# A decoder layer on one core: final norm's column sums addend by addend, one output tile on another queue, and a new order of all instructions

## The chip, the cores and the metric

The kernel runs on one core of a Trainium2 chip. Times are device microseconds (us) of a whole execution; the profile's own span is from the first to the last instruction. The engines are TensorE (PE, with its weight loads as PEld), VectorE (DVE), ScalarE (ACT), GpSimd (POOL) and SyncE (SP), which only issues transfers; ACT and POOL issue transfers as well, in the same row as their other instructions.

## The reference, cut to what matters

One layer over 512 tokens with model width 1024, float32 throughout:

```python
h = h + 0.5 * swiglu(rmsnorm(h, ffn1_norm), ffn1_w_gate, ffn1_w_up, ffn1_w_down)
proj = rmsnorm(h, mix_norm) @ w_in                # u, v, z, xbc, dt
ya = rmsnorm(chunked_spatial_gating(gelu(u), gelu(v), ...), gm_out_norm)
yb = mamba2_mixer(z, xbc, dt, ...)                # causal conv, SSD in chunks of 128, gated norm
h = h + concatenate([ya, yb], -1) @ w_out
h = h + 0.5 * swiglu(rmsnorm(h, ffn2_norm), ffn2_w_gate, ffn2_w_up, ffn2_w_down)
gate = sigmoid(rmsnorm(h, ple_norm) @ ple_w_gate + ple_b_gate)
h = h + gate * (p @ ple_w_proj)
return rmsnorm(h, final_norm)                     # y * rsqrt(mean(y*y) + eps) * gain, per token
```

## The kernel before, in words

The layer is held feature by feature: `h` is eight tiles of 128 features x 512 tokens. Large products are made in float32r, of which the trace records one pass for each matmul and not two as for float32: each float32 operand is split into a high and a low float32r part (`whi`, `wlo` for weights; ACT casts the high part, DVE subtracts it to get the low one), and a product is three float32r matmuls, high by high, high by low, low by high. In the FFNs and the mixer, products are 256 columns (half the tokens) or 512 wide. Small products stay float32: the column sums over features against a tile of ones, the transposes against `ident`, the causal convolution and the state-space part of the mixer (`convin`, `m`, `u`). PE's row is a mixture of the two.

The end of the kernel: the gate of the per-layer embeddings is a product for each of eight feature tiles d. For the last three, d = 5, 6, 7 (`BY_HALF = 3`), it is made by halves of the tokens, A and B, 256 each (`gate_half`, line 1842). Behind each, DVE and ACT apply the sigmoid and the embedding, add to `h`, square it (`sq`), and scale `h` by the final gain. `factors` (line 1850) adds four squares (that of d 0 to 4 together, `total`, which is the tile `ssum`, and d 5, 6, 7) over the features by 128x1 matmuls into one PSUM bank, and makes the factors of a half (`rlast`) from it with a square root on ACT and some short DVE steps. `rows_out` (line 1864) transposes `h` back to rows, four 128x128 transposes to a bank, eight banks in all; ACT evicts the banks with q = 0, DVE those with q = 1, each scaling by `rlast`, and ACT's queue sends ACT's tiles, SP's queue DVE's.

No engine's order follows from the code. All instructions are recorded first, cut into units (a PE unit is the run of matmuls into one bank), and issued in the order of the string `ORDER`, a list of the units' numbers. So what stands next to what on each engine, and each place in a queue, is set by that list, and every recorded instruction has the line of `issue` (1905) in the profile. `b` and `a` are PSUM banks.

Of the kernel before, what the change touches and what calls it, by code (L numbers as in the profile page):

```python
# [76 lines left out]
for _name, _w in _VECS:  # L77
# [211 lines left out]
def layer_kernel(ctx: ExitStack, tc: tile.TileContext, a: dict, out: bass.AP):  # L289
# [93 lines left out]
    def sm_ps(at=None):  # L383
        return bank()
# [1457 lines left out]
    def gate_half(i, tok):  # L1842
# [4 lines left out]
        gained(d, tok)  # L1847
        return sq

    def factors(tok, sqs):  # L1850

        chunks = range(tok.start // P, tok.stop // P)
        ps = sm_ps()
# [24 lines left out]
    for i in range(BY_HALF):  # L1878
        squares_of[0].append(gate_half(i, halves[0]))
# [133 lines left out]
```

## Time and profile before

| | before |
|---|---|
| median of 3 runs | 1074.15 us (1074.07 to 1074.2) |
| profiled execution | 1073.36 us |
| its span | 1071.6 us |
| TensorE's granted clock, mean | 0.999 |
| PE busy | 1062.1 us (99%) |
| DVE busy | 817.0 us (76%) |
| ACT busy | 559.5 us (52%) |
| POOL busy | 75.2 us (7%) |

The profiled execution is one run by itself; its time is the span and what lies around it. PE's busy time counts a matmul from its start to its modelled end, and successive matmuls overlap, so that 99% says that PE has no holes, not that it works at its peak.

### The profile page before, as it was taken

How to read it: one execution, taken by the hardware profiler on the slowest of the kernel's cores; microseconds unless marked ns; L12 is line 12 of the kernel's file. 1: busy time of each engine (PE TensorE's matmuls, PEld its weight loads, DVE VectorE, ACT ScalarE, POOL GpSimd, SP SyncE). 2: the span in 40 equal slices, each digit the busy share in tenths (PEclk: the TensorE clock that was granted, in tenths of full speed). 3: DMA queues.
4: the chain of work that ended last, by engine and by line, in shares of the span. 5: the costliest groups of instructions: out<-in, count | busy, mean ns of one | idle time of the engine just before them, and what ended most of it. 6: DMA issues, size and time to landing. Idle time of an engine off the chain costs nothing.

```text
span 1071.6 us, 17611 instructions
## 1 busy us (share of the span) xinstructions
PE 1062.1 (99%) x7151; PEld 965.0 (90%) x7151; DVE 817.0 (76%) x1169; ACT 559.5 (52%) x781; POOL 75.2 (7%) x95
## 2 busy tenths in 40 slices
PE   9999999999999999999999999999999999999997
PEld 7899999999998878998999888999999999999887
DVE  6978685867577879999999767988667575857866
ACT  7655344444444537887865435654434343534545
POOL 1100000100000000000100000010100000000000
PEclk9999999999999999999999999999999999999999
DMA  9876765766452236777855435786755757633412
GB/s 322 238 202 166 196 181 193 196 181 174 99 154 82 65 113 146 187 201 175 212 135 130 138 98 137 218 236 186 204 143 155 211 144 197 181 115 85 139 53 79
DMA packets 52209, 173.27 MB, mean 162 GB/s; under 512 B 5920, under 2 KB 6176, under 8 KB 52128
## 3 DMA queue, kind: packets, MB, share of 16 engines
q1 hardware_dynamic: 33696, 116.93, 32.1%
q0 software_dynamic: 12256, 44.57, 23.1%
q10 hardware_dynamic: 6176, 10.65, 3.4%
q8 instruction: 56, 0.92, 0.3%
q14 instruction: 25, 0.20, 0.1%
HBM read 167.86 MB, written 4.26 MB: 161 GB/s over the span
## 4 chain that ended last, share of the span: by engine, by line
PE 99%; DVE 0%; ACT 0%; issue 0%; DVEq 0%; ACTq 0%
PE b L1905 81%; PE a L1905 18%; DVEq L2008 0%; DVE o L1905 0%; ACT m L1905 0%; ACT b L1905 0%; DVE tmp L1905 0%; DVE h L1905 0%; DVE ones L410 0%; DVE nv L1905 0%; ACTq L1905 0%
## 5 line engine op out<-in xcount | busy, mean ns | idle before, releaser
L1905 PE MATMUL b<-xfb,whi 128*128 128x256 f32 (+1 forms) x1704 | 297.5, 278 | 0.7 <-ACT b L1905 0.7
L1905 PEld LDWEIGHTS b<-xfb,whi 128*128 128x128 f32 x1704 | 261.0, 188 | 6.0 <-ACT b L1905 0.9
L1905 PE MATMUL b<-xfb,wlo 128*128 128x256 f32 (+1 forms) x852 | 237.2, 278 | 0.0
L1905 ACT CAST whi<-raw 128x1024 fp32r<-128x1024 f32 (+1 forms) x131 | 136.0, 1041 | 146.4 <-PE b L1905 109.7
L1905 DVE TENSOR_TENSOR wlo<-raw,whi 128x1024 fp32r<-128x1024 f32 (+1 forms) x130 | 156.8, 1212 | 28.7 <-ACT whi L1905 25.8
L1905 PEld LDWEIGHTS b<-xfb,wlo 128*128 128x128 f32 x852 | 159.9, 188 | 0.5
L1905 PE MATMUL b<-xfa,whi 128*128 128x256 f32 (+1 forms) x696 | 124.0, 281 | 0.0
L1905 PEld LDWEIGHTS b<-xfa,whi 128*128 128x128 f32 x696 | 107.0, 188 | 2.5 <-DVE xfa L1905 0.2
L1905 PE MATMUL b<-xfa,wlo 128*128 128x256 f32 (+1 forms) x348 | 97.8, 281 | 0.0
L1905 ACT CAST whix<-rawd 128x1024 fp32r<-128x1024 f32 (+1 forms) x40 | 39.4, 986 | 88.5 <-PE a L1905 47.9
L1905 DVE TENSOR_TENSOR wlo<-rawb,whi 128x1024 fp32r<-128x1024 f32 x51 | 62.1, 1220 | 23.2 <-ACT whi L1905 23.1
L1905 ACT CAST whi<-rawb 128x1024 fp32r<-128x1024 f32 x51 | 53.3, 1049 | 48.8 <-PE b L1905 39.7
L1905 PE MATMUL b<-m,whi 128*128 128x512 f32 x224 | 69.6, 392 | 0.0
L1905 DVE TENSOR_TENSOR wlox<-rawd,whix 128x1024 fp32r<-128x1024 f32 (+1 forms) x40 | 45.7, 1143 | 27.0 <-ACT whix L1905 26.9
L1905 PEld LDWEIGHTS b<-xfa,wlo 128*128 128x128 f32 x348 | 65.4, 188 | 0.5
L1905 PE MATMUL b<-xb,whi 128*128 128x256 f32 (+1 forms) x280 | 62.2, 318 | 0.0
L1905 PE MATMUL b<-ghi,wlox 128*128 128x512 f32 x156 | 61.4, 394 | 0.0
L1905 PE MATMUL b<-glo,whix 128*128 128x512 f32 x156 | 61.2, 392 | 0.0
L1905 PE MATMUL b<-ghi,whix 128*128 128x512 f32 x156 | 60.7, 389 | 0.0
L1905 PE MATMUL a<-ghi,wlox 128*128 128x512 f32 x140 | 55.2, 394 | 0.0
L1905 PE MATMUL a<-glo,whix 128*128 128x512 f32 x140 | 54.9, 392 | 0.0
L1905 PE MATMUL a<-ghi,whix 128*128 128x512 f32 x140 | 54.4, 389 | 0.0
(294 smaller groups left out, 2223.8 us busy)
## 6 DMA issues: line engine op xcount, KB each, us to landing
raw<-in_ffn_gu SPq DMA_DIRECT2D x57, 512.0 KB, 5.4
rawd<-in_ffn_down SPq DMA_DIRECT2D x40, 512.0 KB, 4.4
raw<-in_ffn_gu POOLq DMA_DIRECT2D x32, 512.0 KB, 7.7
rawb<-in_ffn_gu SPq DMA_DIRECT2D x31, 512.0 KB, 6.1
s<-in_ffn_gu SPq DMA_DIRECT2D x21, 512.0 KB, 5.5
s<-in_ffn_gu POOLq DMA_DIRECT2D x21, 512.0 KB, 8.5
raw<-in_w_out SPq DMA_DIRECT2D x16, 512.0 KB, 3.6
raw<-in_w_in SPq DMA_DIRECT2D x13, 512.0 KB, 3.7
```

The costliest lines, as they stand in the source:

```text
L1905: getattr(getattr(real, engine), what)(*(real_of(x) for x in args), **{k: real_of(x) for k, x in kw.items()})
```

## The change

It does three things. First, the column sums: each half gets its bank ahead of the loop, `total` is added at once, and each gate half's square is added behind its product (`column_sums`); `factors` only makes the factors. Second, `rows_out` sends the last tile that DVE evicts (chunk 3, q = 1) from ACT's queue and not from SP's. Third, `ORDER` is replaced as a whole by another list that a search has found, in which a change from float32 to float32r (or back) on PE carried a charge. The list's numbers tell a reader nothing and are left out, but for its first line:

```diff
 ORDER = (
-    "1-2 5-7 9-10 13 12 11 3 14 16 18 20 24 15 17 19 0 25 21 77 26 41 27 29 42 38 37 39-40 34 8 35 43 33 "
...
+    "1-2 5-7 9-10 13 12 11 0 3 14 16 18 24 20 15 17 19 25 21 26 41 78 27 29 42 37-38 40 39 8 43 32 36 "
...
@@ -1847,16 +1848,14 @@
         gained(d, tok)
         return sq
 
-    def factors(tok, sqs):
-
-        chunks = range(tok.start // P, tok.stop // P)
-        ps = sm_ps()
-        for j, sq in enumerate([total[:, tok]] + sqs):
-            for i in range(len(chunks)):
-                nc.tensor.matmul(
-                    ps[:, i : i + 1], sq[:, i * P : (i + 1) * P], ones[:, 0:1], start=i + j == 0,
-                    stop=j == len(sqs) and i == len(chunks) - 1, skip_group_check=True,
-                )
+    def column_sums(ps, sq, first, last):
+        for i in range(2):
+            nc.tensor.matmul(
+                ps[:, i : i + 1], sq[:, i * P : (i + 1) * P], ones[:, 0:1], start=first and i == 0,
+                stop=last and i == 1, skip_group_check=True,
+            )
+
+    def factors(ps):
         rt = sb("rlast", (P, 2))
         rsqrt_by_table(rt, ps[:, :2], 1.0 / D, (P, 2))
         return rt
@@ -1872,17 +1871,16 @@
                     nc.scalar.activation(o, ps, AF.Copy, scale=rt[:, i : i + 1])
                 else:
                     nc.vector.tensor_scalar(o, ps, rt[:, i : i + 1], None, ALU.mult)
-                (nc.sync if q else nc.scalar).dma_start(out[c * P : (c + 1) * P, q * T : (q + 1) * T], o)
-
-    squares_of = [[], []]
+                (nc.sync if q and c < NC - 1 else nc.scalar).dma_start(out[c * P : (c + 1) * P, q * T : (q + 1) * T], o)
+
+    sums = [sm_ps(), sm_ps()]
+    for k, tok in enumerate(halves):
+        column_sums(sums[k], total[:, tok], True, False)
     for i in range(BY_HALF):
-        squares_of[0].append(gate_half(i, halves[0]))
-    for i in range(BY_HALF):
-        if i == BY_HALF - 1:
-            r_a = factors(halves[0], squares_of[0])
-        squares_of[1].append(gate_half(i, halves[1]))
-    rows_out(halves[0], r_a)
-    rows_out(halves[1], factors(halves[1], squares_of[1]))
+        for k, tok in enumerate(halves):
+            column_sums(sums[k], gate_half(i, tok), False, i == BY_HALF - 1)
+    rows_out(halves[0], factors(sums[0]))
+    rows_out(halves[1], factors(sums[1]))
```

The instructions are the same in number and kind on every engine. Three places show how the list moves them.

On PE in the mixer, in the convolution's part, before: a group of four `convin` matmuls (float32; each number after a name is that of a buffer) stands behind float32r products, with two float32r matmuls against `onesr` behind it.

```order
L1905 MATMUL b_6001<-xb_3482,whi_5911 128x256 x2
L1905 MATMUL b_6001<-xb_3482,wlo_5932 128x256
L1905 MATMUL b_6026<-convin_5070,m_5463 128x128
L1905 MATMUL b_6026<-convin_5070,m_5581 128x128
L1905 MATMUL b_6026<-convin_5070,m_5390 128x128
L1905 MATMUL b_6026<-convin_5070,m_5388 128x128
L1905 MATMUL b_6031<-tmp_5779,onesr_73 128x512
L1905 MATMUL b_6031<-tmp_5936,onesr_73 128x512
```

Now, from the same place: the two `onesr` matmuls come first, and seven groups of `convin` stand in one piece, 28 matmuls without a float32r product among them.

```order
L1903 MATMUL b_5995<-xb_3477,whi_5909 128x256 x2
L1903 MATMUL b_5995<-xb_3477,wlo_5929 128x256
L1903 MATMUL b_6020<-tmp_5873,onesr_73 128x512
L1903 MATMUL b_6020<-tmp_5935,onesr_73 128x512
L1903 MATMUL b_6023<-convin_5155,m_5468 128x128
L1903 MATMUL b_6023<-convin_5155,m_5391 128x128
...
L1903 MATMUL b_6096<-convin_5519,m_5706 128x128
L1903 MATMUL b_6096<-convin_5519,m_5700 128x128
L1903 MATMUL b_5995<-xb_3474,whi_6040 128x256 x2
L1903 MATMUL b_5995<-xb_3474,wlo_6059 128x256
```

Before, these seven groups stood in pieces of 4, 12 and 12, each behind 24 products or more. Another four `convin` follow later at the same place in both.

On PE at the very end, before: behind the last product come the sums of half A, then 16 transposes (left out), then the sums of half B, then the rest.

```order
L1905 MATMUL b_10793<-x_10224,wlo_10691 128x256
L1905 MATMUL b_10854<-ones_71,ssum_10670 128x1 x2
L1905 MATMUL b_10854<-ones_71,sq_10395 128x1 x2
L1905 MATMUL b_10854<-ones_71,sq_10397 128x1 x2
L1905 MATMUL b_10854<-ones_71,sq_10398 128x1 x2
L1905 MATMUL b_10878<-ident_65,h_91 128x128
...
L1905 MATMUL b_10893<-ident_65,h_98 128x128
L1905 MATMUL b_10898<-ones_71,ssum_10670 128x1 x2
L1905 MATMUL b_10898<-ones_71,sq_10396 128x1 x2
L1905 MATMUL b_10898<-ones_71,sq_10874 128x1 x2
L1905 MATMUL b_10898<-ones_71,sq_10870 128x1 x2
L1905 MATMUL b_10921<-ident_65,h_97 128x128
```

Now the sums of B follow those of A, and all 32 transposes stand behind both. The product ahead of them is in both d 7's of half B.

```order
L1903 MATMUL b_10819<-x_10216,wlo_10686 128x256
L1903 MATMUL b_10844<-ones_71,ssum_10666 128x1 x2
L1903 MATMUL b_10844<-ones_71,sq_10403 128x1 x2
L1903 MATMUL b_10844<-ones_71,sq_10406 128x1 x2
L1903 MATMUL b_10844<-ones_71,sq_10405 128x1 x2
L1903 MATMUL b_10878<-ones_71,ssum_10666 128x1 x2
L1903 MATMUL b_10878<-ones_71,sq_10404 128x1 x2
L1903 MATMUL b_10878<-ones_71,sq_10866 128x1 x2
L1903 MATMUL b_10878<-ones_71,sq_10872 128x1 x2
L1903 MATMUL b_10887<-ident_65,h_91 128x128
```

On ACT at the end, before: evictions (`o<-b`) and issues of the output (`out<-o`) alternate, and an eviction stands ahead of the issue of its tile; ACT issues only what it evicts. `ACT_TABLE_LOAD` readies the square root.

```order
L1905 ACT_TABLE_LOAD
L1905 ACTIVATE ny_10872<-nv_10866 128x2
L1905 ACTIVATE sq_10874<-h_96 128x256
...
L1905 ACTIVATE o_10400<-b_10883,rlast_141 128x512
L1905 DMA out<-o_10400 128x512
L1905 ACTIVATE ny_10917<-nv_10912 128x2
L1905 ACTIVATE o_10401<-b_10878,rlast_141 128x512
L1905 DMA out<-o_10401 128x512
L1905 ACTIVATE o_10405<-b_10888,rlast_142 128x512
L1905 ACTIVATE o_10406<-b_10926,rlast_142 128x512
L1905 DMA out<-o_10405 128x512
L1905 DMA out<-o_10406 128x512
```

Now the table load stands behind the last square, and the issue of `o_10411`, which DVE evicts as its last, stands behind the second eviction, ahead of two evictions and three issues of ACT's own.

```order
L1903 ACTIVATE sq_10866<-h_97 128x256
L1903 ACT_TABLE_LOAD
L1903 ACTIVATE ny_10875<-nv_10869 128x2
...
L1903 ACTIVATE o_10407<-b_10887,rlast_141 128x512
L1903 DMA out<-o_10407 128x512
L1903 ACTIVATE o_10412<-b_10897,rlast_142 128x512
L1903 DMA out<-o_10411 128x512
L1903 ACTIVATE o_10413<-b_10926,rlast_141 128x512
L1903 DMA out<-o_10412 128x512
L1903 DMA out<-o_10413 128x512
L1903 ACTIVATE o_10414<-b_10936,rlast_142 128x512
L1903 DMA out<-o_10414 128x512
```

What moved: one issue that stood on SP, and the table load by one instruction. On SP the four issues of the output become three.

## Rows read from the trace of the kernel before

**Rows 1.** The page, whole span: busy time by engine; last chain by engine.

```profile
PE 1062.1 (99%) x7151; PEld 965.0 (90%) x7151; DVE 817.0 (76%) x1169; ACT 559.5 (52%) x781; POOL 75.2 (7%) x95
...
PE 99%; DVE 0%; ACT 0%; issue 0%; DVEq 0%; ACTq 0%
```

**Rows 2.** The chain of waits: start us, length us, what the end hangs on.

```profile
12.78 14.01 PE b L1905 x60
...
553.33 0.59 ACT m L1905
...
678.76 0.58 ACT b L1905
...
1005.54 57.18 PE b L1905 x346
...
1065.87 0.66 DVE o L1905
```

**Rows 3.** Timeline of PE at 553 and 679 us; idle time in brackets.

```profile
553.96 0.51 PE L1905 MATMUL a<-xa,whi 128*128 128x256 f32 x2 [0.26 <-ACT m L1905]
...
679.38 0.52 PE L1905 MATMUL b<-xfb,whi 128*128 128x256 f32 x2 [0.66 <-ACT b L1905]
```

**Rows 4.** Timeline of PE in the mixer: start us, length us, instruction, count.

```profile
562.13 0.28 PE L1905 MATMUL a<-xb,wlo 128*128 128x256 f32 x1
...
562.25 1.05 PE L1905 MATMUL b<-convin,m 128*128 128x128 f32 x8
...
563.05 0.48 PE L1905 MATMUL b<-xb,whi 128*128 128x256 f32 x2
...
563.37 0.28 PE L1905 MATMUL b<-xb,wlo 128*128 128x256 f32 x1
...
565.49 0.28 PE L1905 MATMUL b<-xb,wlo 128*128 128x256 f32 x1
...
569.34 0.28 PE L1905 MATMUL b<-xb,wlo 128*128 128x256 f32 x1
...
571.38 0.28 PE L1905 MATMUL b<-xb,wlo 128*128 128x256 f32 x1
```

**Rows 5.** Table by stretches, PE alone: stretch, length, busy (matmuls), clock, DMA.

```profile
401.00:427.00 26.00, 26.00 (x113) 1.00 0.59 144
595.00:610.00 15.00, 15.00 (x68) 1.00 0.52 147
```

**Rows 6.** Timeline of PE behind the last product, 1057 to 1065 us.

```profile
1057.37 0.50 PE L1905 MATMUL b<-ones,ssum 128*128 128x1 f32 x4
...
1059.08 1.95 PE L1905 MATMUL b<-ident,h 128*128 128x128 f32 x16
...
1060.86 0.50 PE L1905 MATMUL b<-ones,ssum 128*128 128x1 f32 x4
...
1062.56 2.29 PE L1905 MATMUL b<-ident,h 128*128 128x128 f32 x16
```

**Rows 7.** Timeline of the other engines and the queues in the tail.

```profile
1059.19 1.28 ACT L1905 ACT_TABLE_LOAD   x1
...
1059.99 0.42 DVE L1905 TENSOR_TENSOR sq<-h 128x256 f32<-128x256 f32 x1
...
1061.58 0.75 DVE L1905 TENSOR_SCALAR o<-b,rlast 128x512 f32<-128x512 f32 x1
...
1064.19 1.27 ACT L1905 ACTIVATE o<-b,rlast 128x512 f32<-128x512 f32 x2 [0.48 <-PE b L1905]
...
1065.49 0.34 ACTq L1905 DMA_DIRECT2D out<-o  x1
...
1066.55 1.06 SPq L1905 DMA_DIRECT2D out<-o  x2
```

**Rows 8.** DMA issues from 1060 us: count, size, median us to landing.

```profile
out<-o ACTq DMA_DIRECT2D x4, 256.0 KB, 2.5
out<-o SPq DMA_DIRECT2D x4, 256.0 KB, 3.0
```

245 rows, old and new, of the table ORDER are left out of this document.

## The prediction

> **What bounds the kernel now.** Three views, in this order. The page's first part says how busy each engine is, its fourth part which engine the end of the program hangs on [rows 1]: TensorE (PE) is busy 99% of the span, and the chain that ended last is 99% PE. So only three things can move the time: the holes in PE's row, the spacing at which PE starts its matmuls, and the stretch behind PE's last product.
>
> The chain of waits lists the holes [rows 2]. From 12.78 us on it is PE, broken only twice: at 553.33, where PE waits for ScalarE's (ACT's) 0.59 us copy of a bank, and at 678.76, for a 0.58 us copy. The timeline gives the same places from PE's side: its next matmul starts with 0.26 and 0.66 us of idle time ahead of it [rows 3]. At the end the chain's last PE product stretch begins at 1005.54 and lasts 57.18 us, to 1062.71; the last link is VectorE's (DVE's) eviction at 1065.87, 0.66 us long.
>
> Spacing is read from start times, since a matmul's own duration overlaps its neighbour's. In the mixer, PE alternates float32r products, 256 columns wide, with small float32 matmuls `b<-convin,m`, each recorded as two passes [rows 4]. From 563.37 to 565.49 PE starts 18 products in 2.12 us, 117.8 ns each; from 569.34 to 571.38 again 18, in 2.04 us, 113.3 ns each. The products are of one kind; float32 groups lie between the two stretches, and one ahead of the first. For products of 512 columns, the table by stretches [rows 5] has 113 in 26 us and 68 in 15 us; less the two that straddle a stretch's edges that is 234 and 227 ns. So PE has two spacings 3 to 4% apart, and a group of float32 is one place at which it passes from one to the other, in both directions.
>
> **The change part by part.** All sums are against the profiled execution: span 1071.6, time 1073.36, 1.76 us around it. The median of the runs shown, 1074.15, is 0.79 above that; differences carry over.
>
> *Column sums addend by addend.* The same eight 128x1 matmuls per half, 16 passes. PE takes 1059.08 - 1057.37 = 1.71 us for half A's and 1062.56 - 1060.86 = 1.70 for half B's [rows 6]. None is added or dropped, and the order fences show that the list still puts all sixteen behind the last product. Cost 0. What changes is their neighbour: B's sums now follow A's, and all 32 transposes come last.
>
> *The tail, from T0 = 1057.37 (the end of the last product).* Sums A end at 1059.08 as before. B's four pairs follow at 0.43 us a pair, so the last pair wants its square at 1059.08 + 3 x 0.43 = 1060.37; in the trace DVE's last square begins at 1059.99 and lasts 0.42, to 1060.41 [rows 7]. So PE waits about 0.05 at most, and B's sums end near 1060.8. Then 32 transposes; the first sixteen took 1060.86 - 1059.08 = 1.78 us [rows 6], so 3.56 in all, to 1064.4. Before, sixteen of them began at 1062.56 and took 2.29, to 1064.85. PE ends 0.45 earlier. That is no gain by itself, since behind it stand the evictions. ACT's table load, 1.28 us from 1059.19 in the trace [rows 7], now stands behind ACT's last square (the order fence), some 0.4 us if it takes as long as DVE's; half A's factors come as much later, so DVE's first eviction starts not at 1061.58 [rows 7] but near 1062.0. DVE has four evictions at about 0.68 each and half B's short steps: the third ends near 1064.4, just when the last transposes do, and the last near 1065.3. The chain's last eviction ended at 1066.53 [rows 2]; this part alone would give 1.2 us.
>
> Then the queues. Before, SyncE (SP) issued the last two tiles from 1066.55, two issues in 1.06 us [rows 7], beside ACT, which was done at 1065.83. Now DVE's last tile is issued by ACT, and the order fence shows where: behind it on ACT stand two evictions and three more issues. ACT waits for DVE's last eviction, to 1065.3; issues, 0.34 [rows 7], to 1065.65; evicts, 0.64 (two took 1.27, in the same rows), to 1066.3; issues twice, the second of them behind that eviction, to 1066.7; evicts, to 1067.35; and issues last at about 1067.4. ACT's tiles landed a median of 2.5 us after their issue, SP's 3.0 [rows 8]. That is 1069.9 to 1070.4. Before, SP's second issue, from about 1066.9, with 3.0 gives 1069.9. So the tail costs 0 to +0.5; I take +0.3, as the last issues stand close together and share the transfer. Were ACT's evictions not held back, the tail would end on DVE's last eviction: 1065.3 + 0.34 + 2.6 = 1068.2, or -1.7. If DVE's work ran 0.4 later than I sum it, +0.9. Bounds -1.7 to +0.9.
>
> A rule bears on this place and would speak for the move: the Trainium skill, "Trainium Kernel Development and Optimization" (Key Constraints), says that transfers issued from several engines' queues run on the same 16 DMA engines, and that spreading them only saves issue time. By it the move is worth at most the SP issue that it takes off the end, 0.68 of the 1.06 us, so about -0.7. The order of ACT's row contradicts that here: the issue saved on SP is paid on ACT with two evictions behind it.
>
> *The list: fewer changes between float32 and float32r.* Counting along PE's row in both orders, float32r is followed by float32 (or a transpose) 34 times before and 30 times after. The price of one change itself is in [rows 4]: product to `convin` 562.25 - 562.13 = 0.12 (spacing 0.113); eight passes and the first product to the third, 563.37 - 562.25 = 1.12; eight passes at 0.112 and two products at 0.113 would be the same 1.12. So the change itself costs 0.01 us, and four of them nothing. What follows it can cost: 4.5 ns a product until the spacing falls back. The float32 groups that the new list merges are followed by 24 to 48 products: 0.11 to 0.22 us each, if slow behind it. At [rows 4] one of three was not. Four by 0.16 by about two thirds is 0.4; I take -0.4, with 0 and -0.9 (all four, at 0.22) for the ends.
>
> *The list: the two holes.* At both places the rows of the changed order keep their neighbours: the same product, the same copy, the next product into that bank. Cost 0; both gone would be -0.9 [rows 3].
>
> *The list: everything else.* Units change places mostly by 3 to 11 us and among their like. At the start PE's chain runs unbroken from 12.78 for 14.01 us [rows 2]; the moved SP load and the later square stay ahead of their first reader there by about 0.6. Work of DVE and ACT is the same, DVE idle a quarter of the span [rows 1]. I put it at 0. Below, a hole costs as [rows 3] shows, 0.3 to 0.7; above, the spacing can fall back elsewhere.
>
> **Sum**: 0 (sums) + 0.3 (tail) - 0.4 (fewer changes) + 0 + 0 = -0.1 against 1073.36; carried to the median, 1074.0.
>
> **The rivals.**
> (a) *The spacing is what the list really moves.* If long stretches now slow run at the fast spacing, each 26 us of 512-wide products [rows 5] gives 26 x 7/234 = 0.8 us, each 26 us of 256-wide ones 26 x 4.5/117.8 = 1.0. For it: both spacings occur for one kind of product, with a float32 group between [rows 4]. Against: the order of the long 512-wide stretches is nearly untouched. Three or four such stretches are -2.5 to -4: 1071.0.
> (b) *New holes.* The other sign. A re-made list puts some split or copy late, and PE, which has no slack, waits as at 679.38, 0.66 us [rows 3]. It decides from four such holes on, +2.6: 1076.7. Against it: only two holes stand in the row of before with work as dense; for it, hundreds of units have moved.
> (c) *The tail turns out a gain*, because ACT's issue does not hold back its evictions for long: by about 1.4 with the fewer changes, 1072.8. The row of ACT is in order in every view here, which speaks against it. By itself this stays within what can be told.
> (d) *The list changes nothing, and the tail costs +0.9*: 1075.0.
>
> **How the numbers follow.** What a measurement of this kernel can tell from no change is about 0.2%, 2.15 us: below 1072.0 is faster, above 1076.3 slower. My forecast 0.53, (a) 0.20, (b) 0.12, (c) 0.08, (d) 0.07. (a) is faster but for a tenth of it, and a forecast joined with (c) reaches there too: faster 0.22. (b) lies above but for a small part: slower 0.11. Same 0.67. The forecast's own range, from the ends of its terms, is 1071.6 (-0.9 - 1.7) to 1075.0 (+0.9); to leave out no more than 2 in 10 it must reach into (a) and to the edge of (b): 1071.0 to 1076.3.
>
> **What would show it.** Right: a PE row without new holes over 0.2 us; the holes near 553 and 679 as they are; sums of 3.4 us back to back behind the last product, transposes of 3.5; ACT idle ahead of its DMA issue until DVE's last eviction, and the last landing some 12.5 to 13 us behind the last product. Wrong: 18 products at 2.04 us over long stretches that had 2.12; or a third row in PE's waits; or evictions on ACT that start before DVE's last has ended.

## The result: 0.19% slower, and the profile after

| | before | changed |
|---|---|---|
| median of 13 runs | 1074.15 us (1073.48 to 1074.72) | 1075.55 us (1073.41 to 1077.29) |
| ratio | | 1.0019, 95% interval 1.0012 to 1.0026 |
| mean granted clock, by run | | 0.995 to 0.999 |
| profiled execution, its span | 1073.36, 1071.6 us | 1075.55, 1073.8 us |

By the ratio the change costs 2.0 us, 0.19% (the medians lie 1.4 apart); the forecast was 1074.0, 0.15 us below before. The time lies inside the forecast's range, but on the other side of no change. The spread says as much as the median: the runs of the changed kernel lie 3.9 us apart, those of before 1.2, and they follow their granted clock, from 1073.41 at 0.999 to 1077.29 at 0.995.

The page of the changed kernel, busy time and the last chain, beside [rows 1]:

```profile
PE 1064.4 (99%) x7151; PEld 966.1 (90%) x7151; DVE 816.9 (76%) x1169; ACT 560.0 (52%) x781; POOL 77.1 (7%) x95
...
PE 98%; ACT 1%; DMA 1%; DVE 0%; SPq 0%; issue 0%; ACTq 0%
```

PE is as busy as before, for 2.3 us more. Its waits, in total, count and longest:

```profile
PE b L1903 <- DVE tmp L1903: 1.7, 1, 1.7
PE b L1903 <- ACT b L1903: 0.7, 1, 0.7
PE b L1903 <- ACT whi L1903: 0.3, 1, 0.3
PE a L1903 <- ACT m L1903: 0.3, 1, 0.3
PE b L1903 <- DVE xfa L1903: 0.2, 1, 0.2
PE b L1903 <- DVE glo L1903: 0.2, 1, 0.2
```

The waits for `tmp`, `b` and `m` were there before; both mid-kernel holes are as they were [rows 3]. The 0.3 us for `whi` lies at 6 us, in the start; it isn't the new list's doing, as a second profile of the kernel before has it too (e12, 0.4 us). The two of 0.2 us don't recur in a second profile of the changed kernel (e11). So there are no new holes of any size, and the time is elsewhere. PE's rows behind the last product (start, length, instruction), beside [rows 6]:

```profile
1058.77 0.50 PE L1903 MATMUL b<-ones,ssum 128*128 128x1 f32 x4
...
1060.48 0.58 PE L1903 MATMUL b<-ones,ssum 128*128 128x1 f32 x4
...
1062.27 5.36 PE L1903 MATMUL b<-ident,h 128*128 128x128 f32 x32
```

The last product ends at 1058.77, 1.40 later than before. The sums of both halves take 3.50 us, nearly as forecast. But the 32 transposes take from 1062.27 to beyond 1067, 5.2 us where the forecast had 3.56. The table by stretches (stretch, its length, PE busy and count, granted clock, DMA share, GB/s) says why:

```profile
1058.80:1062.30 3.50, 3.50 (x35) 1.00 0.00 0
1062.30:1063.00 0.70, 0.70 (x8) 1.00 0.00 0
1063.00:1066.70 3.70, 3.70 (x22) 0.54 0.38 142
```

In 3.70 us behind 1063 the granted clock is 0.54: it has fallen from its full level, 2.4 GHz, to the half one, 1.2, for nearly all of it. There 16 transposes start 213 ns apart; before, and in the 0.7 us ahead, 109. That is 16 x 0.104 = 1.7 us. Ahead of the fall PE was busy without a gap, with sums of one column and then a few transposes. The last chain, beside [rows 2]:

```profile
1067.66 0.76 DVE o L1903
1068.44 0.34 ACTq L1903
...
1068.84 0.70 ACT o L1903
1069.55 0.34 ACTq L1903
...
1069.94 0.69 ACT o L1903
```

This is the queue that the prediction worked out: ACT issues DVE's last tile at 1068.44, right behind DVE's eviction, and only then evicts, issues, evicts.

So two parts: the last product comes 1.40 later, and the tail, from there to the end of the span, is 15.1 us long and not 14.3.

### The profile page after: what moved, and what is told of

Its sections match the earlier page's. It is cut to its first block, busy times and chain, and to the rows that moved or that the text cites. A ratio compares the mean times of both kernels' runs of the same rounds, so it can differ in the third digit from the quotient of the medians.

```text
span 1073.8 us, 17623 instructions
## 1 busy us (share of the span) xinstructions
PE 1064.4 (99%) x7151; PEld 966.1 (90%) x7151; DVE 816.9 (76%) x1169; ACT 560.0 (52%) x781; POOL 77.1 (7%) x95
## 4 chain that ended last, share of the span: by engine, by line
PE 98%; ACT 1%; DMA 1%; DVE 0%; SPq 0%; issue 0%; ACTq 0%
PE b L1903 80%; PE a L1903 18%; DMA h<-in_x 1%; ACT xfa L1903 0%; ACT whi L1903 0%; ACT o L1903 0%; ACT ghi L1903 0%; DVE xfa L1903 0%; SPq L1903 0%; DVE o L1903 0%; ACTq L1903 0%; ACT m L1903 0%; ACT b L1903 0%; ACT tmp L1903 0%
```

## The experiments

Their times, with ratios to the kernel before in the same session, and where PE stood. The last six columns are differences, in us, between the starts of the same pass (one recorded matmul) of PE's row (numbers 300, 2700, 3450, 4200 and 4950, counted from 0, and the first column sum of half A or, with 128 columns, its place) in this profile and in the first one of before, where they are at 58.01, 428.91, 517.35, 624.28, 741.34 and 1057.37.

| kernel | median (range) | ratio, 95% interval | clock by run | 58 | 429 | 517 | 624 | 741 | 1057 |
|---|---|---|---|---|---|---|---|---|---|
| changed | 1075.55 (1073.41 to 1077.29) | 1.0019 (1.0012 to 1.0026) | 0.995 to 0.999 | 0.43 | 0.66 | 1.70 | 1.24 | 1.34 | 1.40 |
| e1_sums_apart | 1074.62 (1074.5 to 1075.22) | 1.0006 (0.9998 to 1.0015) | 0.998 to 0.999 | -0.10 | 0.13 | 1.70 | 1.38 | 1.48 | 1.54 |
| e2_sums_together | 1076.66 (1076.03 to 1077.97) | 1.0027 (1.0016 to 1.0039) | 0.996 to 0.998 | 0.29 | 0.29 | 0.47 | 0.47 | 0.47 | 0.47 |
| e3_tile_on_sp | 1074.80 (1073.85 to 1075.77) | 1.0007 (0.9998 to 1.0016) | 0.995 to 0.998 | 0.10 | 0.33 | 1.36 | 0.70 | 0.80 | 0.86 |
| e4_stretches_back | 1075.86 (1073.36 to 1076.62) | 1.0011 (1.0003 to 1.0020) | 0.995 to 0.999 | 0.14 | 0.14 | 0.22 | -0.18 | -0.08 | -0.02 |
| e5_best | 1072.85 (1072.07 to 1074.36) | 0.9994 (0.9985 to 1.0003) | 0.998 to 0.999 | 0.18 | 0.17 | 0.17 | -0.15 | -0.90 | -0.84 |
| e6_u_in_one | 1074.07, one run | | 0.998 | -0.12 | 0.11 | 0.94 | 0.57 | -0.19 | -0.13 |
| e7_518_to_620 | 1072.88, one run | | 0.999 | 0.09 | 0.09 | 0.28 | -0.12 | -0.12 | -0.12 |
| e8_sums_before_last | 1080.55 (1077.98 to 1080.66) | 1.0058 (1.0045 to 1.0070) | 0.993 to 0.998 | 0.04 | 0.28 | 1.32 | 0.66 | 0.76 | |
| e9_wide_sums | 1072.77 (1072.48 to 1073.03) | 0.9994 (0.9985 to 1.0003) | 0.998 to 0.999 | 0.26 | 0.49 | 1.56 | 1.17 | 0.42 | 0.48 |
| e10_wide_best | 1072.81 (1072.3 to 1073.59) | 0.9996 (0.9987 to 1.0005) | 0.998 to 0.999 | -0.09 | -0.10 | 0.08 | -0.19 | -0.94 | -0.88 |
| e11_changed_again | 1075.03, one run | | 0.997 | -0.12 | 0.11 | 1.14 | 0.69 | 0.79 | 0.85 |
| e12_before_again | 1073.03, one run | | 0.998 | 0.30 | 0.31 | 0.29 | 0.28 | -0.35 | -0.36 |

Theory 1 is that the clock in the tail falls because the sums of both halves now stand together; theory 2, that the list makes PE late and that is all.

**Sums apart, in the changed kernel.** In its list the four units of half B's sums go behind half A's transposes:

```diff
- 2650 2666 2682 2698 2711 2708 2723 2714 ... 2705 2726 2729 2732
+ 2711 2708 2714 2705 2650 2666 2682 2698 ... 2723 ... 2726 2729 2732
```

> The changed kernel, with the column sums of half B behind half A's sixteen transposes again, as before; nothing else moves. Theory 1 (the tail's clock): in the changed kernel the granted clock falls to 0.50 at 1063 us, behind 3.9 us of 128x1 sums and a few transposes, and 16 transposes take 213 ns in place of 109, which is 1.7 us. With the sums apart the clock stays at 1.00 to the last transpose, the time falls by 1 to 2 us on the mean, to about 1074, and its runs lie within about 1 us of each other, not 4. Theory 2 (the list: PE's last product ends 1.40 us later than before, and that alone is the loss): the time stays at 1075.5.

The runs lie 0.7 us apart. The table by stretches of its tail, to the last transpose:

```profile
1058.90:1062.40 3.50, 3.50 (x35) 1.00 0.00 0
1062.40:1066.00 3.60, 3.60 (x34) 1.00 0.00 0
```

The clock is 1.00 throughout, although its last product ended later still than the changed kernel's (1.54 behind before). Theory 1 holds for the spread and, by the ratios, for 1.3 of the 2 us (1.0019 to 1.0006; the two intervals just overlap); the rest is left for the list and the queue.

**Sums together, in the kernel before.** Unit 2710 goes behind 2684, and ACT's square 2682 ahead of its square root 2686.

> The kernel before, with half B's sums directly behind half A's (and ACT's last square ahead of the square root, so that they needn't wait); the rest of its list is kept. Theory 1: the granted clock falls in the tail, in some runs earlier than in others, the runs spread over some 4 us, and their mean is 1 to 2 us above the kernel before. Theory 2: the time of the kernel before, 1074, or a little less, since PE's wait of 0.3 us among the transposes is gone.

It is 0.27% slower than before, with a granted clock of 0.996 or 0.997 in six of its seven runs (0.998 or 0.999 in all of before). The stretches: sums of both halves, with a wait of 0.53 us that the edit brought in; then some ten transposes; then the fall, with a second wait of 0.53 us among the last transposes:

```profile
1057.90:1062.00 4.10, 3.57 (x33) 1.00 0.00 0
1062.00:1063.00 1.00, 1.00 (x11) 1.00 0.00 0
1063.00:1066.50 3.50, 2.97 (x16) 0.53 0.27 99
```

So the loss of clock moves with the order of the sums from one kernel to the other. The waits make this a weaker proof of its size: they cost by themselves, too.

**The last tile on SP, in the changed kernel.**

```diff
-(nc.sync if q and c < NC - 1 else nc.scalar).dma_start(...)
+(nc.sync if q else nc.scalar).dma_start(...)
```

> The changed kernel with its last VectorE tile sent by SP's queue again. By the prediction's term for the tail (ACT waits with its issue for DVE's last eviction, with two evictions of its own behind it), ACT's last evictions start at once, the last issue comes 1 to 2 us earlier, and the time falls by 0.3 to 1.5 us. Rival: the end hangs on the transposes at half clock and on the transfers, and the queue of the one tile changes less than 0.2.

1.0007 against 1.0019, some 1.3 us, though the intervals overlap. In the profile ACT's last two evictions wait for PE and no longer for DVE, and the end comes 13.9 us behind the last product and not 15.1, with a clock that fell as in the changed kernel (whose second profile, e11, has 15.1 again). The queue is a cost, as worked out.

```profile
1065.51 0.69 ACT L1896 ACTIVATE o<-b,rlast 128x512 f32<-128x512 f32 x1 [0.76 <-PE b L1896]
...
1066.68 0.69 ACT L1896 ACTIVATE o<-b,rlast 128x512 f32<-128x512 f32 x1 [0.49 <-PE b L1896]
```

**Three stretches of the list back.** The changed list, with the pieces of before's from place 1 to 747 and 996 to 1391 (of 2735), where both hold the same units.

> The changed kernel, with the order of before in three stretches of the list: up to 78 us, 78 to 333 us, and 429 to 518 us, over which the changed kernel's PE fell behind by 0.42, 0.24 and 1.04 us. Theory 2 (the list): the last product ends 1.7 us earlier than in the changed kernel, about 0.3 earlier than before, and the time falls by 1.7 to about 1073.8, with a tail that still loses its clock and runs that spread as widely. Theory 1 alone: no change, 1075.5.

The last product is back at 1057.35, as before, where -0.3 was expected. By the ratios the time fell by 0.9 us, half of what was expected, but the intervals overlap and the medians (1075.86, and 1075.55 for the changed kernel) show no fall. The runs lie 3.3 us apart, most of them with a lower clock (1073.36 at 0.999, 1076.62 at 0.996), so that what the list alone is worth can't be told from their times. This profile happens to be one with the clock at 1.00, and shows the queue by itself:

```profile
1064.57 0.76 DVE o L1896
1065.35 0.34 ACTq L1896
...
1065.75 0.70 ACT o L1896
1066.46 0.34 ACTq L1896
...
1066.85 0.69 ACT o L1896
```

**A version put together from these.** e4's list, the last tile on SP, the sums apart, and half A's factors and evictions ahead of half B's:

```diff
- ... 2650 2666 2682 2698 2711 2708 2723 2714 2701-2702 2717 2703-2704 2718 2712-2713 ...
+ ... 2711 2708 2714 2705 2650 2666 2682 2698 2701-2704 2712-2713 2709 2717-2718 ...
```

> A version from what the first four runs showed: the changed kernel with the order of before in the three stretches of the earlier run, the last VectorE tile on SP's queue, and in the tail sums A, half A's transposes, sums B, half B's transposes, with half A's factors and evictions ahead of half B's on DVE and ACT. If the clock theory and the term for the queue hold, the clock is 1.00 to the last transpose, the end comes about 12.3 us behind the last product (14.2 before), and the time is 1071.5 to 1072.5, faster than before. If the tail hangs on something else, 1073.5 to 1074.5.

The median is 0.7 below before's in its session, and the interval reaches to 1.0003, so faster is not shown. The clock held; the end came 13.8 us behind the last product, not 12.3.

**The groups of 64 columns in one piece.** Units 1170 and 1149 go ahead of 1169, in the changed list. In the changed kernel, near 465 us:

```profile
463.08 1.58 PE L1903 MATMUL b<-u,m 128*64 128x128 f32 x16
464.59 1.60 PE L1903 MATMUL b<-m,m 128*128 128x128 f32 x12
466.12 1.58 PE L1903 MATMUL b<-u,m 128*64 128x128 f32 x16
```

and in e4, with the order of before there:

```profile
462.82 0.83 PE L1896 MATMUL b<-m,m 128*128 128x128 f32 x6
463.58 2.57 PE L1896 MATMUL b<-u,m 128*64 128x128 f32 x32
```

32 passes of 64 columns take 2.57 us in one piece, and 2 x 1.58 in two.

> The changed kernel, with one piece of its list as before: the two groups of eight float32 matmuls with 64 columns near 465 us (b<-u,m) stand in one piece again, and two groups of 128-column float32 matmuls ahead of them and not between them. Theory: the groups of 64 columns start closer together as long as they follow each other, and going into and out of them costs 0.3 us or so a time; then the stretch of PE from 449 to 482 us, which took 1.0 to 1.3 us longer in the changed kernel and in two of its versions, is shorter by 0.5 to 0.8. Rival: the changes between float32 and float32r or the spacing behind them carry the difference, and it shrinks by less than 0.2.

From 429 to 517 PE lost 0.83 and not 1.04: a gain of 0.2, where 0.5 to 0.8 was expected. In one piece, the 32 passes took 3.01 us here from their first start to the next product's, as much as in two (2 x 1.51), and not the 2.50 of e4: the last 13 starts were no closer than 0.109 us. Their order alone isn't it, and this theory falls. Swapping the whole stretch back does recover it (e4, e5, e10: 0.08, 0.00 and 0.18).

**The stretch from 518 to 620 us alone, in the kernel before.**

> The kernel before, with the changed list in the stretch from 518 to 620 us alone (there the seven convin groups are merged). In the changed kernel and three versions of it this stretch of PE was 0.3 to 0.7 us shorter. By the prediction's term (products behind a float32 group at 118 and not 113 ns), it is 0.3 to 0.5 shorter here too; if the gain came from what stood ahead of the stretch, 0.

The column from 517 to 624 says 0.40 shorter. All of it is gained between 562 and 587 us, where the `convin` groups stand. The rows from the first of 24 products to the `convin` group behind them, in before and here:

```profile
577.34 0.40 PE L1905 MATMUL a<-xb,whi 128*128 128x256 f32 x2
...
580.17 1.06 PE L1905 MATMUL b<-convin,m 128*128 128x128 f32 x8
```

```profile
577.41 0.39 PE L1899 MATMUL a<-xb,whi 128*128 128x256 f32 x2
...
580.13 1.05 PE L1899 MATMUL b<-convin,m 128*128 128x128 f32 x8
```

That is 118 ns a product before and 113 now. The term for the merged `convin` groups holds.

**Half A's sums ahead of the last product.** Units 2649, 2658, 2674 and 2690 ahead of 2691, with the squares and `ssum` moved ahead.

> The changed kernel, with the four column sums of half A ahead of the last product (and the squares that they need ahead of their place on DVE and ACT); half B's sums and all 32 transposes stay together behind it. Theory 1 (sums of both halves in one piece let the clock fall): the granted clock stays at 1.00 to the last transpose, and the runs lie within about 1 us of each other, at about 1074. Rival (32 small transposes in a row, or the end of the program, let it fall): the transposes run at 213 ns as in the changed kernel, and the runs spread over 3 us or more.

It went the other way, 0.58% slower. The edit made PE wait 0.96 us for `ssum`, and the clock then fell behind the sums of one half. Stretches: the wait, the sums, most of the last product, and from the last sums to near the end of the transposes:

```profile
1055.40:1056.40 1.00, 0.07 (x1) 1.00 0.00 0
1056.40:1058.30 1.90, 1.87 (x17) 0.98 0.00 0
1058.60:1061.60 3.00, 3.00 (x15) 0.50 0.02 5
1065.30:1071.60 6.30, 6.30 (x30) 0.50 0.24 90
```

The clock fell as the last product began, came back, and fell again within a second wait, of 1.2 us, behind three of half B's four pairs of sums. So "both halves together" is too narrow: here a wait and sums of one half stood ahead of each fall, and this run doesn't say which of the two did it. The rival of this run isn't supported either, as the products themselves ran at half clock.

**The same sums with 128 columns.** One edit to the changed kernel, its list untouched:

```diff
-ps[:, i : i + 1], sq[:, i * P : (i + 1) * P], ones[:, 0:1], ...
+ps[:, i * P : (i + 1) * P], sq[:, i * P : (i + 1) * P], ones, ...
-rsqrt_by_table(rt, ps[:, :2], 1.0 / D, (P, 2))
+rsqrt_by_table(rt, ps[:, 0 : P + 1 : P], 1.0 / D, (P, 2))
```

> The changed kernel, its list untouched, with each column-sum matmul against 128 columns of ones and not one (the bank takes 128 equal columns, of which the factors read one); the same number of matmuls, which should start at the same 0.11 us a pass, as other float32 passes of 128 columns do. Theory 1a (the sums of one column leave the array nearly idle, and that is what lets the clock fall behind two halves of them): the granted clock stays at 1.00 to the last transpose, no transpose takes 213 ns, and the runs lie within about 1 us of each other, at 1073.5 to 1074.5. Rival 1b (the fall comes from the stretch without large float32r products, 7 us long, whatever its matmuls are): it falls as in the changed kernel, with 1075.5 and a spread of 3 us or more.

Its tail, by stretches and in PE's rows:

```profile
1057.90:1061.40 3.50, 3.50 (x33) 1.00 0.00 0
1061.40:1064.80 3.40, 3.40 (x33) 1.00 0.27 99
```

```profile
1057.85 0.61 PE L1896 MATMUL b<-ones,ssum 128*128 128x128 f32 x4
...
1061.42 3.66 PE L1896 MATMUL b<-ident,h 128*128 128x128 f32 x32
```

The sums take 3.57 us (3.50 with one column), at the same places and just as close together, and the transposes 3.5 and not 5.2. The runs lie 0.55 us apart. With everything else in place, the width of the sums' operand made the difference: with 128 columns the clock stayed at its full level, with one column it fell. How long PE's row goes without a large product is the same in both, so that isn't it.

**All of it together.** The 128-column sums in e4's list with the tile on SP:

> The sums of 128 columns together with the three stretches of before's order and the last VectorE tile on SP's queue, with the changed kernel's own order in the tail. If theory 1a holds, all three losses are gone at once: clock 1.00, last product at about 1057, the end about 12.4 us behind it (14.2 before), a time of 1071 to 1072. If 1b holds, 1073 to 1076 with a wide spread.

No better than the one edit, though the last product came 1.36 earlier than in e9. The tail is 14.4 us long, where 12.4 was expected. Its issues are done at 1065.0; count, size and time from issue to landing:

```profile
out<-o ACTq DMA_DIRECT2D x4, 256.0 KB, 4.0
out<-o SPq DMA_DIRECT2D x4, 256.0 KB, 3.7
```

Before, these were 2.5 and 3.0 [rows 8]. Eight tiles are now issued within 3.3 us, and landing takes longer; that the transfers themselves bound this tail is likely, and wasn't tried.

**The two kernels once more.**

> The changed kernel itself, profiled once more, to tell the list from what differs between executions. If the list sets it all, the start (0.54 us behind the kernel before at 37 us) and the stretch from 680 to 741 us (118 ns a product) are as in its first profile. If executions differ, as the earlier versions suggest (the start lay anywhere from 0 to 0.5 behind, and the same products between 680 and 741 us took 0.75 less with an untouched list), they come out otherwise, while the stretch from 448 to 481 us stays 0.9 to 1.3 us longer than in the kernel before.

> The kernel before, profiled once more, for the same question: the start and the stretch from 680 to 741 us may differ from its first profile by some tenths of a microsecond, the stretch from 448 to 481 us by no more than 0.3, and no transpose takes 213 ns.

One list gives different starts (0.43 and -0.12; 0 and 0.30) and different spacings from 624 to 741 us (the kernel before gained 0.63 there in its second profile, e9 0.85 against the changed kernel, with the same list). The 429 to 517 us loss is there each time: 1.04, 1.03, and -0.02 in the kernel before. The tail repeats, too: the transposes take 5.2 us again in e11, and run at full clock in e12.

## Why the prediction was wrong

**The step that failed** is the first: "Column sums addend by addend ... Cost 0. What changes is their neighbour." The neighbour was the cost. Sums behind sums leave PE with 3.5 us of one-column matmuls, behind which the granted clock fell to its half level; the transposes took 5.2 us and not "3.56 in all", so of the prediction's signs "transposes of 3.5" failed. The prediction took the trace's full clock in the tail as given, though [rows 6] hold transposes between the two halves' sums, and priced the move by PE's busy time alone. None of its rivals was this. Its size is best read from the end of the last issue of an output tile, against the last product: 12.2 us behind it in both profiles of the changed kernel, 10.6 in e4 and e9, which have the same order there at full clock. So the fall of the clock costs 1.6 us of the tail. The times say 1.3 (e1) and 2.7 us (e9, whose ratio is 0.9994), with intervals of 0.7 to 1.0 us either way; part of e9's is not the clock, as its last product comes 0.92 us earlier, 0.85 of it by the spacing from 624 to 741 us that differs between executions of one list. The last issues (changed, e4, e9):

```profile
1070.66 0.34 ACTq L1903 DMA_DIRECT2D out<-o  x1
...
1067.57 0.34 ACTq L1896 DMA_DIRECT2D out<-o  x1
...
1068.12 0.34 ACTq L1896 DMA_DIRECT2D out<-o  x1
```

The Trainium skill, "TensorE: Matmul & The Clock Gate" (Part 1: The HAM clock gate), says that a hardware monitor sets the array's clock by how busy PE has been lately, with half rate for an idle one. That the clock has two levels agrees with the stretches above (1.00, and 0.50 in e8). But the trace had PE busy 3.50 of 3.50 us ahead of the fall in the changed kernel, so the busy share of PE's row in the profile didn't announce it.

**The tail's queue** was right as a mechanism and nearly right in time. Predicted from DVE's last eviction on: 1065.3, 1065.65, 1066.3, 1066.7, evicted by 1067.35; e4, at full clock with the last product at the same place, shows 1065.33, 1065.70, 1066.44, 1066.80, 1067.54. The term was +0.3, and the end of the last issue does come 0.3 to 0.4 us later behind the last product: 10.6 (e4, e9) and not 10.24 [rows 6, 7]. The landing varied more than that: the end came 14.3 us behind the last product in e4, as before, and 13.5 in e9, whose tiles landed sooner (medians of 2.2 and 2.3 us from issue on the two queues, 2.8 and 3.0 in e4); why is open. Taking the tile back to SP gained 1.3 by the ratios and 1.1 in the tail (e3), where the prediction had put 2.0 between its own term and an unblocked ACT (+0.3 and -1.7).

**Fewer changes, -0.4:** right where it was worked out (e7: 0.40 shorter, 0.45 in both profiles of the changed kernel). But "everything else" at 0, without a row for it, is the second step that failed: from 429 to 517 us the new list costs 1.03 us of PE or more in every profile that has it there unedited (1.57 in e1, where more products ran at the slow spacing), and 0.23 from 58 to 429 (0.00 and -0.01 with the old order, e4 and e5). This is rival (b) in small, except that no row calls it a wait. e4 places it in that stretch; what in it costs is only partly known. 0.5 us are the 64-column groups that start further apart (3.0 us in all and not 2.5), and why they do is open (e6).

**The two holes** stayed, as forecast. **The spacing** of rival (a) isn't the list's doing in its large part: one and the same list runs a stretch at either spacing.

So on the whole, in both profiles of the changed kernel PE loses 0.97 us from 58 us to the last product, against the first profile of before: 0.23, then 1.04 lost, 0.45 won, and 0.16 more lost behind 624 us. The tail loses 0.8 more (15.1 us and not 14.3): its order would have won between 0 (e4) and 0.8 (e9) at full clock, and the fallen clock takes that and more. Together that is 1.8 us, near the 2.0 of the ratio; and the clock spreads single runs over 3.9.

## What to carry to other kernels

Before moving small matmuls next to each other, look in PE's row at what they separate: here a stretch of one-column matmuls, with PE busy throughout, was followed by half the clock. Read the granted clock by stretches, and its spread by run, before looking for a late instruction; one operand widened from 1 to 128 columns, at 0.07 us of PE's time in all, took the spread from 3.9 to 0.55 us. And an issue that waited for another engine held all that stood behind it in its queue: those times could be worked out to 0.2 us from an order and a handful of durations, though not when the tiles land.

## What the runs showed of the hardware

- The granted clock fell to its half level (0.54 over 3.70 us) with PE's row 100% busy, behind 128x1 float32 sums that start 0.11 us apart, and didn't with the same sums at 128 columns, which start 0.11 us apart as well (changed, e9).
- It fell as a run of full products began, too, behind a wait of 0.96 us and 1.8 us of such sums (e8).
- The same program ran the same products at 118 or at 113 ns apart in different executions; from 624 to 741 us that was 0.63 us (before and e12), and 0.85 with one list (changed and e9).
- Groups of 64-column float32 matmuls took 2.5 or 3.0 us for 32 passes in one piece (e4, e6), with no wait recorded to tell them apart.
- Eight output tiles of 256 KB issued within 3.3 us landed a median of 4.0 and 3.7 us behind their issue (e10), against 2.5 and 3.0 when issued within 5.3 us (before).
